# The second block's convolution placed tap by tap among the gate/up products of a two-block transformer kernel

## The chip, the cores and the metric

The kernel runs on one core of a Trainium2 chip. The metric is the device time of one execution in microseconds. The core's engines work from queues of their own, each in order: TensorE (PE, matmuls; PEld its weight loads), VectorE (DVE), ScalarE (ACT), GpSimd (POOL), and SyncE (SP), which issues the DMAs here.

## The reference

Two transformer blocks of depth 1 over 1024 tokens of width 1024, in float32. Both end in a gated feed-forward layer with D_FF = 2816 = 22 x 128:

```python
# first block
h2 = modulate(rms_norm(x, g_pre_ffn), shift_f, scale_f)
ff = (silu(h2 @ w_ffn_gate) * (h2 @ w_ffn_up)) @ w_ffn_down
# second block: a causal depthwise convolution of width 3 over the tokens between up and gate
hn = rms_norm_2(h, ffn_norm_pre)
up = causal_dwconv(hn @ w_up, conv_w, conv_b)      # y[t] = b + h[t-2]*w[0] + h[t-1]*w[1] + h[t]*w[2]
g, u = split(up, 2)
ffn = (silu(g) * u) @ w_down
```

Ahead of it stand the mixers (attention and an mLSTM in the first block, retention and sparse attention in the second), which the change does not touch.

## The kernel before

`dense` (L164) is the output projection and the feed-forward layer; it is called twice, with `conv=False` for the first block ("of1") and `conv=True` for the second ("of2"). float32 products are made from rounded parts: every operand is split into a high part (`whi`, a rounded copy made by ScalarE, L357) and a remainder (`wlo`, the difference, L358, made by the engine that the call names), and three matmuls give one product.

Gate and up are computed together, one tile f of 128 gate and 128 up columns at a time, f = 0 to 21. A tile is a 2 x 2 block product by seven multiplications in place of eight (sums of weight blocks times sums of token blocks). Multiplication m takes 12 matmuls of 512 columns; the order is 1, 6, 5, 7, 2, 3, 4, and each of these is a *slot*. The weights of the seven (`prep`, L330) need four sums on VectorE (`ws`, L344). The results lie in three PSUM banks per tile: A holds products 1 and 2, B holds 6, 7 and 4, and Z holds 5 and 3. Product 3 is added into Z, and it is the product whose moving operand is the tile `xq`. Banks are read in between by `after_product` (L380): after product 6, `u2 = t1 + B`; after product 7, `w = t1 + B` and `craw1(odd) = w + Z`; after 3, `craw0(odd) = u2 + Z`; after 4, `craw1(even) = t1 + B`. All four are VectorE additions of L378. `craw0` is the gate half before the convolution and `craw1` the up half; each is one buffer, with 512 of its elements from even and 512 from odd blocks of 128 tokens.

For the second block the convolution of tile g = f - 1 runs beside the products of tile f. `conv_start` (L437) is ScalarE's part: the newest tap with the bias, into `cv`. `conv_taps` (L443) adds the other two taps on VectorE (L448) and, for the gate half, calls SiLU on ScalarE (L450). `conv_end` (L452) multiplies the halves on VectorE (L454) and sends the result to memory (`h_d`) by SyncE. `cv0` and `cv1` have one buffer each.

The order of the work on TensorE, VectorE, ScalarE and GpSimd is the order in which the code issues it. A slot's body first issues `after_product` of the slot before, then a list of further work (`pre[i]` of slot i), then its own matmuls. In `pre`, `q(f, m, engine)` is `prep` with the engine of the remainder. With the convolution, the remainders of product 3 of this tile and of products 5 and 2 of the next are on VectorE, and the other four on GpSimd.

```python
            for fn in post:
                fn()
            post.clear()
            for fn in pre:
                fn()
            multiply(f, m, c, special)
            post.append(lambda: after_product(f, m, special, c))
```

After tile 21 follows the down projection, `down`, over groups of two tiles, a step per block of 128 tokens; its first steps issue the rest of tile 21's convolution through `tail` (L582). In the last tile's lists stand pieces of the down weights (L913) and of the first hidden tiles (L518) in place of the next tile's weights.

Of the kernel before, what the change touches and what calls it, by code (L numbers as in the profile page):

```python
# [23 lines left out]
ALU = mybir.AluOpType  # L24
# [3 lines left out]
S = 1024  # L28
D = 1024
NT = S // P  # L30
KT = D // P
NF = 22
# [8 lines left out]
C_CONV2W, C_CONV2B = 0, 3 * 2 * NF  # L41
# [45 lines left out]
class Builder:  # L87
# [76 lines left out]
    def dense(self, name, bigs, held, w0, names, x_src, x_mid, x_dst, rows, rows2, conv, ahead=None):  # L164
# [10 lines left out]
        nc = self.nc  # L175
# [8 lines left out]
        raws = []  # L184
# [3 lines left out]
        def fetch(kind, i, lags, **kw):  # L188
            W[kind, i] = self.weights_later(steps, src(kind, i), lags, **kw)
# [5 lines left out]
        def run(slots):  # L195
            for slot in slots:
                steps.run(early=True)
                slot()
                steps.run()
                steps.now += 1  # L200
# [124 lines left out]
        def raw_load(f):  # L325
            pl, tag = (px, "wx") if f % 2 else (self.wp, "raw")
            raw[f] = pl.tile([P, 2048], F32, tag=tag, bufs=1, name=tag)
            nc.sync.dma_start(raw[f], src("gu", f))
# [108 lines left out]
        def conv_start(f, j):  # L437
            col = j * NF + f
            cv = tt[f]["cv", j] = pools["v"].tile([P, S], F32, tag=f"cv{j}", bufs=1, name="cv")
            nc.scalar.activation(cv, raws[j][:, 2:], AF.Identity, scale=self.cols[:, C_CONV2W + 4 * NF + col : C_CONV2W + 4 * NF + col + 1],  # L440
                                 bias=self.cols[:, C_CONV2B + col : C_CONV2B + col + 1])

        def conv_taps(f, j):  # L443
            col = j * NF + f
            cv = tt[f]["cv", j]
            for i in (1, 0):
                wc = self.cols[:, C_CONV2W + i * 2 * NF + col : C_CONV2W + i * 2 * NF + col + 1]
                nc.vector.scalar_tensor_tensor(cv, raws[j][:, i : i + S], wc, cv, op0=ALU.mult, op1=ALU.add)  # L448
            if j == 0:
                nc.scalar.activation(cv, cv, AF.Silu)  # L450

        def conv_end(f):  # L452
            g, u = tt[f]["cv", 0], tt[f]["cv", 1]
            nc.vector.tensor_tensor(out=g, in0=g, in1=u, op=ALU.mult)  # L454
            nc.sync.dma_start(h_d[f], g)

        for tb, ps in held.items():
# [8 lines left out]
        q = lambda f, m, eng=nc.gpsimd: lambda: prep(f, m, eng)  # L466
        v = nc.vector
# [14 lines left out]
        def slot(f, m, pre=(), c=slice(0, HALF), special=False):  # L482
            def body():
# [8 lines that stand above are left out]
            return body  # L492
# [18 lines left out]
        order = (1, 6, 5, 7, 2, 3, 4)  # L511
        groups, hidden = {}, {}

        def hid_piece(f, c, hraw, eng):
            hi, lo = (hidden[f][:, i, c * HALF : (c + 1) * HALF] for i in range(2))
            s = hraw[:, c * HALF : (c + 1) * HALF]
            nc.scalar.activation(hi, s, AF.Copy)
            eng.tensor_tensor(out=lo, in0=s, in1=hi.bitcast(F32), op=ALU.subtract)  # L518
# [6 lines left out]
        def early_hid(f):  # L525
            hr = self.rows.tile([P, S], F32, tag="row", name="hraw")
            nc.sync.dma_start(hr, h_d[f])
            groups[f] = hr

        for f in range(1, NF):  # L530
            pre = [[] for _ in range(7)]
            if conv:
                g = f - 1
                pre[0] += [lambda g=g: conv_start(g, 0)]
                pre[1] += [lambda g=g: conv_taps(g, 0), lambda g=g: conv_start(g, 1)]
                pre[2] += [lambda g=g: conv_taps(g, 1)]
                pre[3] += [lambda g=g: conv_end(g)]
            if f == 1:
                pre[0] += [q(1, 2), q(1, 3), q(1, 4)]
            else:  # L540
                pre[0] += [q(f, 3, v if conv else nc.gpsimd), q(f, 4)]
            if f + 2 < NF:
                pre[1] += [lambda f=f: raw_load(f + 2)]
            if f + 1 < NF:
                for i in range(5):
                    pre[2 + i] += [q(f + 1, order[i], v if conv and i in (2, 4) else nc.gpsimd)]
            else:
                pre[1] += [lambda: [early_hid(i) for i in range(3)]]
                pre[2] += [lambda: fetch("dn", 0, (1, 2, 3, 4), lo_engine=lambda i: v if i % 2 else nc.gpsimd)]
                pre[3] += [first_hidden, lambda: hid_piece(0, 0, groups[0], v)]  # L550
                pre[4] += [lambda: hid_piece(0, 1, groups[0], nc.gpsimd), lambda: hid_piece(1, 0, groups[1], v)]
                pre[5] += [lambda: hid_piece(1, 1, groups[1], nc.gpsimd)]
                pre[6] += [lambda: early_hid(3)]
            run([slot(f, m, pre[i]) for i, m in enumerate(order)])


        f = NF - 1
# [20 lines left out]
        def both(gs, tb):  # L578
            for c in range(2):
                down(gs, tb, c)  # L580

        def tail(i):  # L582

            for fn in post:
                fn()
            post.clear()
            if conv:
                if i == 0:
                    conv_start(f, 0)
                    conv_taps(f, 0)  # L590
                    conv_start(f, 1)
                elif i == 1:
                    conv_taps(f, 1)
                    conv_end(f)
                    eso.close()
            if i == 1:
                esx.close()
                self.end_pool = pools["c"] = pools["o"] = self.pool(eso, name + "d")

# [15 lines left out]
        g = (G - 2, G - 1)  # L615
        rows2v = []
        for n in range(G - 2):
            fetch("dn", n + 1, range(4, 8))
            if n == 0:
                for i in range(4):  # L620
                    steps.at(1 + i, lambda i=i: hid_piece(2 + i // 2, i % 2, groups[2 + i // 2], v if i % 2 else nc.gpsimd), early=True)
                steps.at(7, lambda: rows2v.extend(rows2()), early=True)
            else:
                hid_later(n + 1, (0, 1, 2, 2, 4, 5))
            run([(lambda n=n, tb=tb: (tail(tb) if n == 0 and tb < 2 else None, both((n,), tb))) for tb in range(NT)])
        hid_later(g[1], (0, 1, 1, 1, 2, 3))

        def finish(tb, xin, row):
# [66 lines left out]
        n = 4  # L695
# [1503 lines left out]
```

## Time and profile before

| | us |
|---|---|
| median of 3 runs | 2982.58 (2982.33 to 2983.03) |
| the profiled execution | 2978.47 |
| its span, first to last instruction | 2976.7 |
| TensorE busy, share of the span | 2773.2, 93% |
| VectorE busy | 1733.9, 58% |
| ScalarE busy | 1148.1, 39% |
| GpSimd busy | 1228.4, 41% |
| mean granted TensorE clock | 0.968 of full speed |

The gate/up stage of the first block lies at about 880 to 1270 us of the span, that of the second at 2232 to 2720. Busy times of TensorE are modelled, since matmuls overlap; the spacing of starts is the better measure. The granted clock is given as a share of full speed (1.00 is 2.4 GHz, half of it 1.2 GHz).

### The profile page before, as it was taken

What the parts mean: (1) busy time and instruction counts of PE and PEld (TensorE: products, weight loads), DVE (VectorE), ACT (ScalarE), POOL (GpSimd) and SP (SyncE); (2) the same over time, 40 slices, a digit from 0 to 9 for tenths busy, and PEclk for the clock granted to TensorE, in tenths of its full rate; (3) what the DMA queues carried; (4) which work ended last, traced back from release to release, by engine and by line L of the source; (5) the groups of instructions that cost most, each with busy time, mean ns of one, the idle gap of its engine ahead of it and who ended that gap; (6) DMA issues with size and microseconds to landing.
All of it is one profiled execution on the core that took longest, in us unless ns stands there. A gap on an engine that the chain in (4) does not pass through costs nothing.

```text
span 2976.7 us, 41535 instructions
## 1 busy us (share of the span) xinstructions
PE 2773.2 (93%) x15792; PEld 2391.2 (80%) x15792; DVE 1733.9 (58%) x3054; ACT 1148.1 (39%) x2364; POOL 1228.4 (41%) x1127
## 2 busy tenths in 40 slices
PE   5899999999879999999989999889979988998998
PEld 5898888889768888888879999878967767776887
DVE  8635524442563344365564977865377777777556
ACT  5653223222242222321245586567343333333112
POOL 5752222244335555533364436486223222224334
PEclk7999999999989999999999999999989999999999
DMA  5112343363222222142231111121232211123322
GB/s 203 40 42 100 113 149 107 112 196 110 107 106 94 84 85 85 71 149 86 92 133 48 44 44 45 40 65 62 78 114 85 78 71 64 64 77 135 106 92 85
DMA packets 86252, 272.60 MB, mean 92 GB/s; under 512 B 9207, under 2 KB 28663, under 8 KB 71974
## 3 DMA queue, kind: packets, MB, share of 16 engines
q1 hardware_dynamic: 86054, 269.97, 25.9%
q8 instruction: 124, 2.03, 0.3%
q14 instruction: 74, 0.61, 0.1%
HBM read 210.15 MB, written 59.79 MB: 91 GB/s over the span
## 4 chain that ended last, share of the span: by engine, by line
PE 65%; DVE 19%; ACT 7%; issue 4%; POOL 4%; DMA 0%; SPq 0%; DVEq 0%; ACTq 0%; POOLq 0%
PE pd L131 12%; PE pd L132 12%; PE pd L133 12%; PE pd L375 11%; PE pa L375 8%; DVE cv L448 5%; ACT tk_junka L1651 2%; DVE ws L344 2%; DVE craw L378 1%; DVE ada_acc L826 1%; DVE xin L228 1%; PE pa L1904 1%; POOL wlo L913 1%; ACT cv L440 1%; PE pd L1877 1%
## 5 line engine op out<-in xcount | busy, mean ns | idle before, releaser
L131 PE MATMUL pd<-whi,big 128*128 128x256 f32 (+2 forms) x1856 | 554.9, 299 | 11.8 <-DVE big L574 3.8
L132 PE MATMUL pd<-wlo,big 128*128 128x256 f32 (+2 forms) x1856 | 543.9, 293 | 8.2 <-POOL wlo L913 8.2
L133 PE MATMUL pd<-whi,big 128*128 128x256 f32 (+2 forms) x1856 | 542.9, 292 | 0.9 <-POOL big L850 0.6
L913 POOL TENSOR_TENSOR wlo<-raw,whi 128x512 fp32r<-128x512 f32 (+1 forms) x254 | 351.6, 1395 | 399.1 <-ACT whi L911 381.4
L131 PEld LDWEIGHTS pd<-whi,big 128*128 128x128 f32 x1856 | 359.6, 194 | 20.8 <-ACT whi L911 4.6
L132 PEld LDWEIGHTS pd<-wlo,big 128*128 128x128 f32 x1856 | 359.9, 194 | 15.8 <-POOL wlo L913 9.9
L133 PEld LDWEIGHTS pd<-whi,big 128*128 128x128 f32 x1856 | 359.2, 194 | 6.4 <-POOL big L850 0.9
L576 DVE TENSOR_TENSOR big<-big,pd 128x512 f32<-128x512 f32 x304 | 207.4, 685 | 174.2 <-PE pd L133 172.2
L131 PE MATMUL pd<-whi,hid 128*128 128x512 f32 x576 | 228.9, 397 | 0.0
L132 PE MATMUL pd<-wlo,hid 128*128 128x512 f32 x576 | 228.3, 396 | 0.0
L133 PE MATMUL pd<-whi,hid 128*128 128x512 f32 x576 | 228.3, 396 | 0.0
L375 PE MATMUL pd<-big,whi 128*128 128x512 f32 (+1 forms) x840 | 200.6, 389 | 0.0
L375 PE MATMUL pa<-big,wlo 128*128 128x512 f32 x816 | 197.0, 390 | 1.7 <-DVE wt L378 1.7
L375 PE MATMUL pa<-big,whi 128*128 128x512 f32 x768 | 186.1, 391 | 1.7 <-ACT wlo L357 0.9
L375 PEld LDWEIGHTS pd<-big,whi 128*128 128x128 f32 x840 | 157.9, 194 | 30.8
L375 PEld LDWEIGHTS pa<-big,wlo 128*128 128x128 f32 x816 | 152.8, 188 | 35.5 <-issue 2.5
L131 PE MATMUL pd<-big,whi 128*128 128x512 f32 x448 | 180.3, 402 | 0.0
L375 PE MATMUL pd<-big,wlo 128*128 128x512 f32 x744 | 178.7, 389 | 0.0
L448 DVE SCALAR_TENSOR_TENSOR cv<-craw,cols,cv 128x1024 f32<-128x1024 f32 x88 | 156.1, 1773 | 37.6 <-ACT cv L440 36.1
L133 PE MATMUL pd<-big,wlo 128*128 128x512 f32 x448 | 175.0, 391 | 0.3 <-POOL wlo L913 0.3
L132 PE MATMUL pd<-big,whi 128*128 128x512 f32 x448 | 174.6, 390 | 0.0
L375 PEld LDWEIGHTS pa<-big,whi 128*128 128x128 f32 x768 | 145.4, 190 | 33.9 <-ACT wlo L357 2.5
(435 smaller groups left out, 5654.7 us busy)
## 6 DMA issues: line engine op xcount, KB each, us to landing
raw<-in_wu SPq DMA_DIRECT2D x87, 1024.0 KB, 4.9
wx<-in_wu SPq DMA_DIRECT2D x22, 1024.0 KB, 4.8
hraw<-of_h SPq DMA_DIRECT2D x44, 512.0 KB, 5.6
row<-in_w_ada SPq DMA_DIRECT2D x32, 512.0 KB, 3.9
x_d<-xin SPq DMA_DIRECT2D x24, 512.0 KB, 2.6
of_h<-wt SPq DMA_DIRECT2D x44, 256.0 KB, 2.0
of_h<-cv SPq DMA_DIRECT2D x22, 512.0 KB, 2.6
ada<-in_w_ada SPq DMA_DIRECT2D x16, 512.0 KB, 8.0
```

Source lines behind the costliest of these rows:

```text
L131: mm(ps, lh, rh, start=start, stop=False)
L132: mm(ps, lh, rl, start=False, stop=False)
L133: mm(ps, ll, rh, start=False, stop=stop)
L228: nc.vector.scalar_tensor_tensor(x, y, r, x, op0=ALU.mult, op1=ALU.add)
L344: nc.vector.tensor_tensor(out=t, in0=a, in1=b, op=op)
L375: nc.tensor.matmul(ps[:, c], l, r, start=first and k == 0 and i == 0, stop=k == 3 and i == 2, skip_group_check=True)
L378: nc.vector.tensor_tensor(out=out, in0=a, in1=b, op=ALU.add)
L440: nc.scalar.activation(cv, raws[j][:, 2:], AF.Identity, scale=self.cols[:, C_CONV2W + 4 * NF + col : C_CONV2W + 4 * NF + col + 1], bias=se ...
L448: nc.vector.scalar_tensor_tensor(cv, raws[j][:, i : i + S], wc, cv, op0=ALU.mult, op1=ALU.add)
L576: nc.vector.tensor_add(a, a, ps)
L913: eng.tensor_tensor(out=w[1][:, c], in0=raw[:, c], in1=w[0][:, c].bitcast(F32), op=ALU.subtract)
L1651: nc.scalar.activation(junk[:, :w], isc[tbs[i]], AF.Sign, scale=-1.0, bias=f[:, i : i + 1], accum_out=cnt[:, i : i + 1])
```

## The change

Only `dense` changes. The convolution's taps are issued one at a time (`conv_tap(f, j, i)`; j is the half, 0 gate and 1 up, i the tap), each in a slot of its own. The first half's start and first tap of tile f are issued in the last slot of the same tile, behind the addition that completes `craw0`; the start of the second half comes ahead of the first half's second tap and SiLU; the product of the halves comes one slot later, behind the addition into `craw1`, and for tile 21 on GpSimd. All remainders of gate/up weights go to GpSimd. The weights of product 3 are issued in slot 1 instead of slot 0 (in both blocks). In the last tile a piece of a hidden tile moves one slot on, and the tail spreads the rest of the convolution over four steps instead of two and closes two pools in the fourth.

```diff
-        def conv_taps(f, j):
+        def conv_tap(f, j, i):
             col = j * NF + f
             cv = tt[f]["cv", j]
-            for i in (1, 0):
-                wc = self.cols[:, ...]
-                nc.vector.scalar_tensor_tensor(cv, raws[j][:, i : i + S], wc, cv, op0=ALU.mult, op1=ALU.add)
-            if j == 0:
+            wc = self.cols[:, ...]
+            nc.vector.scalar_tensor_tensor(cv, raws[j][:, i : i + S], wc, cv, op0=ALU.mult, op1=ALU.add)
+            if (j, i) == (0, 0):
                 nc.scalar.activation(cv, cv, AF.Silu)
...
-            nc.vector.tensor_tensor(out=g, in0=g, in1=u, op=ALU.mult)
+            (nc.gpsimd if f == NF - 1 else nc.vector).tensor_tensor(out=g, in0=g, in1=u, op=ALU.mult)
...
             if conv:
                 g = f - 1
-                pre[0] += [lambda g=g: conv_start(g, 0)]
-                pre[1] += [lambda g=g: conv_taps(g, 0), lambda g=g: conv_start(g, 1)]
-                pre[2] += [lambda g=g: conv_taps(g, 1)]
-                pre[3] += [lambda g=g: conv_end(g)]
+                if g == 0:
+                    pre[0] += [lambda: conv_start(0, 0), lambda: conv_tap(0, 0, 1)]
+                pre[0] += [lambda g=g: conv_start(g, 1), lambda g=g: conv_tap(g, 0, 0)]
+                pre[1] += [lambda g=g: conv_tap(g, 1, 1)]
+                pre[2] += [lambda g=g: conv_tap(g, 1, 0)]
+                pre[4] += [lambda g=g: conv_end(g)]
+                pre[6] += [lambda f=f: conv_start(f, 0), lambda f=f: conv_tap(f, 0, 1)]
...
-                pre[0] += [q(f, 3, v if conv else nc.gpsimd), q(f, 4)]
+                pre[0] += [q(f, 4)]
+                pre[1] += [q(f, 3)]
...
-                    pre[2 + i] += [q(f + 1, order[i], v if conv and i in (2, 4) else nc.gpsimd)]
+                    pre[2 + i] += [q(f + 1, order[i])]
...
-                pre[4] += [lambda: hid_piece(0, 1, groups[0], nc.gpsimd), lambda: hid_piece(1, 0, groups[1], v)]
-                pre[5] += [lambda: hid_piece(1, 1, groups[1], nc.gpsimd)]
+                pre[4] += [lambda: hid_piece(0, 1, groups[0], nc.gpsimd)]
+                pre[5] += [lambda: hid_piece(1, 0, groups[1], v), lambda: hid_piece(1, 1, groups[1], nc.gpsimd)]
...
-            if conv:
-                if i == 0:
-                    conv_start(f, 0)
-                    conv_taps(f, 0)
-                    conv_start(f, 1)
-                elif i == 1:
-                    conv_taps(f, 1)
+            if conv and i == 0:
+                conv_start(f, 1)
+                conv_tap(f, 0, 0)
+            elif conv and i < 3:
+                conv_tap(f, 1, 2 - i)
+            elif i == 3:
+                if conv:
                     conv_end(f)
                     eso.close()
-            if i == 1:
                 esx.close()
...
-            run([(... tail(tb) if n == 0 and tb < 2 else None ...)])
+            run([(... tail(tb) if n == 0 and tb < 4 else None ...)])
```

On VectorE, in the middle of the second block's gate/up stage, these rows lead up to the addition into `craw1` that product 3 waits for (the last row). `cv` with `craw0` or `craw1` is a tap, `ws` a weight sum, `whi` or `wlo` a remainder, `wt` with `pa` one of the additions `u2` and `w`. Before, from the gate half's taps on:

```order
L358 TENSOR_TENSOR whi_22387<-ws_22388,whi_22387 128x512
L448 SCALAR_TENSOR_TENSOR cv_22385<-craw0_20973,cols_74,cv_22385 128x1024 x2
L378 TENSOR_TENSOR wt_22429<-wt_22407,pa_22416 128x512
L448 SCALAR_TENSOR_TENSOR cv_22412<-craw1_20974,cols_74,cv_22412 128x1024 x2
L454 TENSOR_TENSOR cv_22385<-cv_22385,cv_22412 128x1024
L344 TENSOR_TENSOR ws_22451<-raw_22279 128x512
L344 TENSOR_TENSOR ws_22453<-ws_22451,raw_22279 128x512
L378 TENSOR_TENSOR wt_22469<-wt_22407,pa_22416 128x512
L378 TENSOR_TENSOR craw1_20974<-wt_22469,pd_22436 128x4x128
```

The same stretch now, from the addition that completes `craw0` on:

```order
L378 TENSOR_TENSOR craw0_20973<-wt_22295,pd_22300 128x4x128
L447 SCALAR_TENSOR_TENSOR cv_22370<-craw0_20973,cols_74,cv_22370 128x1024
L378 TENSOR_TENSOR craw1_20974<-wt_22272,pa_22282 128x4x128
L447 SCALAR_TENSOR_TENSOR cv_22370<-craw0_20973,cols_74,cv_22370 128x1024
L447 SCALAR_TENSOR_TENSOR cv_22388<-craw1_20974,cols_74,cv_22388 128x1024
L344 TENSOR_TENSOR ws_22411<-wx_22144,ws_22316 128x512
L378 TENSOR_TENSOR wt_22430<-wt_22408,pa_22417 128x512
L447 SCALAR_TENSOR_TENSOR cv_22388<-craw1_20974,cols_74,cv_22388 128x1024
L344 TENSOR_TENSOR ws_22449<-raw_22280 128x512
L344 TENSOR_TENSOR ws_22451<-ws_22449,raw_22280 128x512
L378 TENSOR_TENSOR wt_22467<-wt_22408,pa_22417 128x512
L378 TENSOR_TENSOR craw1_20974<-wt_22467,pd_22436 128x4x128
```

The remainders are gone from VectorE, the gate half's first tap stands directly behind the addition into `craw0`, and the product of the halves (L454, now L453) no longer stands ahead of the last row.

On ScalarE, the same tile from the copy of bank A into `craw0` (L408) to the up half's bias part. `cv` with `craw0` or `craw1` is a bias part, `cv<-cv` the SiLU, `whi` or `wlo` the rounded copy of a weight, `wt` the copy of product 1. Before:

```order
L408 ACTIVATE craw0_20973<-pd_22394 128x4x128
L357 ACTIVATE whi_22472<-ws_22488 128x512
L357 ACTIVATE wlo_22505<-raw_22279 128x512
L440 ACTIVATE cv_22521<-craw0_20973,cols_74 128x1024
L357 ACTIVATE wlo_22505<-ws_22523 128x512
L357 ACTIVATE whi_22527<-raw_22279 128x512
L386 ACTIVATE wt_22543<-pd_22530 128x512
L450 ACTIVATE cv_22521<-cv_22521 128x1024
L440 ACTIVATE cv_22548<-craw1_20974,cols_74 128x1024
```

Now:

```order
L408 ACTIVATE craw0_20973<-pd_22395 128x4x128
L357 ACTIVATE whi_22472<-ws_22488 128x512
L440 ACTIVATE cv_22505<-craw0_20973,cols_74 128x1024
L357 ACTIVATE wlo_22508<-raw_22280 128x512
L440 ACTIVATE cv_22524<-craw1_20974,cols_74 128x1024
L449 ACTIVATE cv_22505<-cv_22505 128x1024
L357 ACTIVATE wlo_22508<-raw_22280 128x512
L386 ACTIVATE wt_22543<-pd_22530 128x512
```

Both bias parts now stand ahead of the SiLU, and the SiLU ahead of the copy of product 1.

## Rows read from the trace of the kernel before

**Rows 1.** Waits of TensorE, 2210 to 2720: us in total, times, longest.

```profile
PE pd L375 <- DVE craw L378: 54.4, 21, 5.5
```

**Rows 2.** Timeline of TensorE, second block: start, us, line, tiles, count, [idle before].

```profile
2240.65 2.88 PE L375 MATMUL pa<-big,whi 128*128 128x512 f32 x12
2243.37 2.88 PE L375 MATMUL pd<-big,whi 128*128 128x512 f32 x12
2248.27 4.61 PE L375 MATMUL pd<-xq,wlo 128*128 128x512 f32 x12 [2.02 <-DVE craw L378]
2252.72 2.92 PE L375 MATMUL pa<-big,wlo 128*128 128x512 f32 x12
...
2271.69 4.61 PE L375 MATMUL pd<-xq,whi 128*128 128x512 f32 x12 [2.45 <-DVE craw L378]
```

**Rows 3.** Timeline of TensorE, first block, one tile.

```profile
903.10 2.96 PE L375 MATMUL pd<-xq,whi 128*128 128x512 f32 x12
905.90 2.90 PE L375 MATMUL pa<-big,wlo 128*128 128x512 f32 x12
...
922.24 2.03 PE L375 MATMUL pd<-xq,whi 128*128 128x512 f32 x8
```

**Rows 4.** Windows: length, busy of PE, PEld, DVE, ACT, POOL, granted clock, DMA, GB/s.

```profile
2268.00:2278.00 10.00, 7.55 (x27) 5.74 (x26) 6.78 (x9) 3.66 (x6) 2.56 (x2) 0.83 0.31 107
2315.00:2325.00 10.00, 7.56 (x33) 5.89 (x32) 7.31 (x11) 4.03 (x6) 2.57 (x2) 1.00 0.13 53
```

**Rows 5.** Timeline around one wait, VectorE and TensorE, second block.

```profile
2403.17 3.52 DVE L448 SCALAR_TENSOR_TENSOR cv<-craw,cols,cv 128x1024 f32<-128x1024 f32 x2 [1.67 <-ACT cv L440]
...
2406.72 1.22 DVE L454 TENSOR_TENSOR cv<-cv 128x1024 f32<-128x1024 f32 x1
...
2409.91 0.69 DVE L378 TENSOR_TENSOR craw<-wt,pd 128x512 f32<-128x512 f32 x1
...
2410.65 3.06 PE L375 MATMUL pd<-xq,wlo 128*128 128x512 f32 x12 [2.44 <-DVE craw L378]
```

**Rows 6.** Timeline of TensorE, the last tile and the tail.

```profile
2712.04 4.92 PE L375 MATMUL pd<-xq,wlo 128*128 128x512 f32 x12 [5.51 <-DVE craw L378]
2716.80 2.93 PE L375 MATMUL pa<-big,wlo 128*128 128x512 f32 x12
...
2731.64 0.50 PE L131 MATMUL pd<-whi,big 128*128 128x512 f32 x1 [3.76 <-DVE big L574]
```

**Rows 7.** Groups by line, 2240 to 2700: count, busy us, mean ns, idle before.

```profile
L440 ACT ACTIVATE cv<-craw,cols 128x1024 f32<-128x1024 f32 x40 | 49.5, 1238 | 39.5 <-DVE craw L378 39.5
L378 DVE TENSOR_TENSOR craw<-wt,pd 128x512 f32<-128x512 f32 x40 | 27.5, 689 | 50.0 <-PE pd L375 42.8 <-ACT whi L357 6.5
L358 POOL TENSOR_TENSOR whi<-ws,whi 128x512 fp32r<-128x512 f32 x20 | 25.7, 1284 | 64.0 <-ACT whi L357 54.3 <-issue 9.7
L454 DVE TENSOR_TENSOR cv<-cv 128x1024 f32<-128x1024 f32 x20 | 24.5, 1225 | 0.7
L358 DVE TENSOR_TENSOR whi<-ws,whi 128x512 fp32r<-128x512 f32 x20 | 20.3, 1016 | 7.3 <-ACT whi L357 7.3
L344 DVE TENSOR_TENSOR ws<-wx 128x512 f32<-128x512 f32 x20 | 13.6, 682 | 0.0
```

**Rows 8.** Timeline, taps of one tile: beside a remainder on GpSimd, and alone.

```profile
2397.21 1.29 POOL L358 TENSOR_TENSOR whi<-raw,whi 128x512 fp32r<-128x512 f32 x1 [6.07 <-ACT whi L357]
2397.25 2.33 DVE L448 SCALAR_TENSOR_TENSOR cv<-craw,cols,cv 128x1024 f32<-128x1024 f32 x1
...
2399.62 1.28 DVE L448 SCALAR_TENSOR_TENSOR cv<-craw,cols,cv 128x1024 f32<-128x1024 f32 x1
```

**Rows 9.** DMA issues, 2240 to 2700: queue, count, KB each, us to landing.

```profile
wx<-in_wu SPq DMA_DIRECT2D x10, 1024.0 KB, 4.9
of_h<-cv SPq DMA_DIRECT2D x20, 512.0 KB, 2.6
```

More of the change, by code (lines that the diff above doesn't have):

```diff
@@ L441, in conv_start @@
                                  bias=self.cols[:, C_CONV2B + col : C_CONV2B + col + 1])
-        def conv_taps(f, j):
+        def conv_tap(f, j, i):
             col = j * NF + f
             cv = tt[f]["cv", j]
-            for i in (1, 0):
-                wc = self.cols[:, C_CONV2W + i * 2 * NF + col : C_CONV2W + i * 2 * NF + col + 1]
-                nc.vector.scalar_tensor_tensor(cv, raws[j][:, i : i + S], wc, cv, op0=ALU.mult, op1=ALU.add)
-            if j == 0:
+            wc = self.cols[:, C_CONV2W + i * 2 * NF + col : C_CONV2W + i * 2 * NF + col + 1]
+            nc.vector.scalar_tensor_tensor(cv, raws[j][:, i : i + S], wc, cv, op0=ALU.mult, op1=ALU.add)
+            if (j, i) == (0, 0):
                 nc.scalar.activation(cv, cv, AF.Silu)
@@ L624, in dense @@
                 hid_later(n + 1, (0, 1, 2, 2, 4, 5))
-            run([(lambda n=n, tb=tb: (tail(tb) if n == 0 and tb < 2 else None, both((n,), tb))) for tb in range(NT)])
+            run([(lambda n=n, tb=tb: (tail(tb) if n == 0 and tb < 4 else None, both((n,), tb))) for tb in range(NT)])
         hid_later(g[1], (0, 1, 1, 1, 2, 3))
```

## The prediction

> **What bounds the kernel now.** I read the page first (TensorE is busy for nearly the whole span, so the question is where it stands still), then the list of who waited for whom in the second block's gate/up stage, then TensorE's timeline of that stage beside the same stage of the first block, and last VectorE's rows around one wait.
>
> In the second block's stage TensorE waits 21 times for one and the same writer, VectorE's addition into `craw` [rows 1]: once for each of the tiles f = 1 to 21, always at the matmuls that read `xq`, which is product 3. Product 3 accumulates into bank Z, and the addition that reads Z for output quadrant 21 (`plus(odd(raws[1]), ...)`, after product 7) must have read it first. The reader is to see two things in the timeline [rows 2]: most products follow each other at 2.72 us, but product 3 begins about 2.45 us late in every tile, and it then often lasts 4.45 us. The first block runs the same seven products without a convolution, and there a tile takes 922.24 - 903.10 = 19.14 us, its product 3 taking 2.80 [rows 3]. So the long product 3 is a second cost of the wait: in a window that holds it the granted clock is 0.83 of full speed, one part of it at 1.2 instead of 2.4 GHz, while TensorE had just stood still; a window with another such wait shows 1.00 [rows 4]. The length of a tile shows that some waits cost the clock and some do not.
>
> Why the addition is late is seen on VectorE [rows 5]: it comes last in a queue of two pairs of taps, the product of the halves and two weight sums, with no pause ahead of it. VectorE is the bound of this stage, and through a chain: the taps wait for ScalarE's bias part, and the next bias part for the taps.
>
> **The change part by part.**
>
> *The loop.* From product 3 of f = 1 at 2248.27 to that of f = 21 at 2712.04 are 20 tiles in 463.77 us [rows 2, 6], 23.19 each. If TensorE never waits, they take 20 x 19.14 = 382.8. That is 80.97 to gain, and whether it comes is a question of one addition: when is `craw1` written? I lay out VectorE's new order with the durations of [rows 7], zero being the end of product 3. Product 4 then ends at 2.72, 1 at 5.44, 6 at 8.16, 5 at 10.88, 7 at 13.60, and product 2 at 16.32, where product 3 wants its bank.
>
> Addition into `craw0` 0.69; ScalarE's bias part 1.24, to 1.93; first tap 1.28, to 3.21; addition into `craw1` 0.69, to 3.90; second tap to 5.18; first tap of the other half to 6.46 (its bias part ran on ScalarE beside the second tap); a weight sum 0.68, to 7.14; then the addition that needs product 6, from 8.16 to 8.84; last tap to 10.12; two weight sums to 11.48; the addition that needs product 7, from 13.60 to 14.28; the addition into `craw1` to 14.97. It is wanted at 16.32. So VectorE is 1.35 us early, and it stands idle twice on the way (1.02 before product 6, 2.12 before product 7). The product of the halves, which stood ahead of this addition, now stands behind it and ends at 16.2; the sum for product 7 follows, to 16.9, and 19.12 starts the next round. Three remainders (1.02 us on average for those cut from a sum) have left VectorE.
>
> *The price of those three on GpSimd.* GpSimd takes 1.28 us for one [rows 7], seven in a tile are 9 of 19.1 us, so it has the time. But the two engines get in each other's way: a tap takes 1.28 us alone and 2.33 beside a remainder on GpSimd [rows 8], 1.05 more. In the stretch to 13.60 stand the remainders of 2, 4, 3 and the next 1, four of them. Without a hit the addition is 1.35 early; if all four hit a tap or a sum it is later by 4.2, less the idle time it finds on the way. Two hits before 8.16 cost 2.10 - 1.02 = 1.08, two more after it 2.10, which ends the sums at 14.66 instead of 11.48, and `craw1` at 16.03, still 0.3 early; a fifth hit, by a remainder left over from the tile before, makes it 17.1, so 0.8 late. I take zero, since five hits in five are not likely and the additions that read PSUM keep their 0.69 throughout [rows 7]; the bound is 0.8 us a tile, and with it the clock again (1.65).
> The Trainium skill (SBUF — State Buffer, "SBUF: two separate sides") speaks against the change here: VectorE and GpSimd share a pair of ports as an exclusive lock, and whoever comes second is blocked for the whole instruction. The trace agrees in kind (1.05 of a 1.29 us instruction); by the rule all seven remainders could block VectorE in turn, which is the first rival below.
>
> *First and last tile.* At f = 1, product 2 starts at 2243.37 and product 3 at 2248.27 instead of 2.72 later: 2.18 to gain [rows 2]. The new order there puts ScalarE's SiLU ahead of three copies for the weights, which can hold the copy of product 1 and with it product 7; from nothing to 1.4 us, an estimate from the taps ahead of it (two at 1.28 to 2.33); I take 0.5. At f = 21, product 3 lasts 4.76 us instead of 2.80: 1.96 to gain [rows 6]. Its wait of 5.51 is inside the 20 tiles. Two instructions on VectorE (a remainder of the down weights, one of the hidden tile) take the place of the sums, 0.68 to 1.73 us each (a sum's time, with a hit or without), which brings `craw1` to 15.0 at best and 17.1 at worst: nothing taken.
>
> *The tail.* Behind f = 21 TensorE waits 3.76 us for a copy out of PSUM that stands behind taps and the product of the halves [rows 6]. The taps are now spread over three steps of 2.72 us with two copies of about 0.69 in each, and the product is on GpSimd. Per step VectorE has 1.4 for the copies, 1.28 to 2.33 for a tap and in two steps 0.7 to 1.7 more: 2.7 to 5.4 against 2.72, with banks for some two steps of delay. The remaining wait lies between 0 and 3.8; I take 2, a gain of 1.8.
>
> *First block.* The remainder for product 3 moves one product later there too, still four products ahead of its use; TensorE has no wait in that stage [rows 3], whose rows follow each other at 2.72 to 2.80. Nothing, with a bound of 1 us either way for the order of GpSimd's work. The later closing of pools at both tails issues nothing; SyncE's queue keeps its order but for one load. Nothing.
>
> Sum: 80.97 + 2.18 - 0.5 + 1.96 + 1.8 = 86.4. The profiled execution took 2978.47, so 2892.1; the median of the runs shown lies 4.1 above it, and the forecast for a median is 2896.
>
> **The rivals.**
>
> *VectorE stays the bound, by GpSimd.* For it: the 2.33 above, three more remainders in a tile, and a VectorE that was the bound. Against it: the 3.1 us of idle time in the layout. VectorE's own work in a tile is four taps 5.12, the product 1.23, four sums 2.72 and five additions 3.45, together 12.5; with seven hits of 1.05 and 1.33 for the first bias part it is 21.2. A tile that long has a wait of 2.1, and with the clock's 1.65 takes 22.9: hardly a gain, 2896 + 20 x 3.7 = 2970. With the bound of four hits (0.8 late) it is 2896 + 16 = 2912, or 2945 where the clock falls too. By the Trainium skill's rule (the page named above), seven whole instructions of 1.29 in place of seven waits of 1.05 give a tile of 24.5, 2896 + 20 x 5.4 = 3004; since no row shows more than 1.05 and most of the trace's remainders meet nothing, that has 0.01 of this rival's chance.
>
> *The output tile's copy to memory.* `cv0` has one buffer. The new bias part of the first half is issued only two products behind the product of the halves, and has to wait until that result is in memory. The copy lands 2.6 us after its issue [rows 9]: 16.2 + 2.6 = 18.8, and the bias part wants to start at 19.12 + 0.69 = 19.8. That is 1.0 us of slack (before, it had two products more). If the weights' load of 1024 KB, 4.9 us [rows 9], ran into it, the copy would land at 23.7, or at 24.7 with a hit on the product; ScalarE would stand 3.9 to 4.9 us with VectorE's first tap behind it, and after the 1.35 of slack product 3 would wait 2.5 to 3.6 us: a tile of 23.3 to 24.4, clock included, against 23.19. The ends give back 5.4, so it is 2979 to 3001, slower from a wait of 2.7 us in every tile; I price it at 3.35, 2996. Against it: by the layout GpSimd has the remainders of 4 and 3 at about 10, when SyncE issues the load, which has landed at 15.
>
> *Little changes.* The wait is only traded for another of the same length (a bank, a weight): 2975 to 2988. The even waits of [rows 1], one writer alone, speak against it.
>
> **How the numbers follow.** The forecast 0.75 (2888 to 2906 by itself: the tail and the first tile between their bounds), VectorE by GpSimd 0.17, the copy 0.03, little changes 0.03, and 0.02 for more than I count. The range, 2889 to 2930, takes in the forecast and the milder half of the first rival. A difference of 0.2% (6 us) is what a measurement here can tell from none: faster 0.95, the same 0.02, slower 0.03.
>
> **What would show it.** Right: in the second block's stage a tile takes 19.1 us, TensorE's list of waits there has no addition into `craw` any more, the granted clock is 1.00, and the addition into `craw1` ends a little over 1 us before product 3. The gaps at 2248 and 2712 are gone; that behind f = 21 is under 3.8. Wrong: `xq` rows that still start late; then taps of 2.3 us standing beside most remainders are the first rival, and a bias part on ScalarE that waits for a copy is the second.

## The result, and the profile after

The changed kernel takes 2893.56 us (median of four runs, 2891.78 to 2897.18) against 2982.57, a ratio of 0.9703 (95% interval 0.9686 to 0.9720). The forecast was 2896. The profiled execution took 2897.18 us, its span is 2895.4.

TensorE's list of waits in the second block's gate/up stage and the stage ahead of it (line waited for: us in total, times, longest) no longer has the 21 waits of [rows 1]:

```profile
PE pd L375 <- ACT wx L357: 5.6, 1, 5.6
PE pa L300 <- DVE big L304: 5.2, 3, 2.5
...
PE pa L375 <- DVE wt L378: 1.7, 2, 0.9
PE pd L375 <- ACT big L303: 1.1, 1, 1.1
PE pd L375 <- DVE big L304: 0.3, 1, 0.3
```

What is left stands in tile 0 and in the turning of the inputs ahead of it. TensorE's timeline (start, us, line, operation, count), at tile 1, at one tile in the middle and at tile 21, answers to [rows 2] and [rows 6]:

```profile
2251.40 2.88 PE L375 MATMUL pd<-big,whi 128*128 128x512 f32 x12
2254.12 3.01 PE L375 MATMUL pd<-xq,wlo 128*128 128x512 f32 x12
2256.97 2.92 PE L375 MATMUL pa<-big,wlo 128*128 128x512 f32 x12
...
2464.74 2.96 PE L375 MATMUL pd<-xq,whi 128*128 128x512 f32 x12
...
2483.88 2.49 PE L375 MATMUL pd<-xq,wlo 128*128 128x512 f32 x10
...
2636.99 3.03 PE L375 MATMUL pd<-xq,wlo 128*128 128x512 f32 x12
2639.86 2.92 PE L375 MATMUL pa<-big,wlo 128*128 128x512 f32 x12
2642.62 0.39 PE L131 MATMUL pd<-whi,big 128*128 128x512 f32 x1
```

Product 3 follows product 2 after 2.72 us everywhere, and the tile in the middle takes 2483.88 - 2464.74 = 19.14 us, as in the first block [rows 3]. From tile 1 to tile 21 it is 2636.99 - 2254.12 = 382.87, where it was 463.77. In the tail TensorE has no wait at all; the list for that stretch is empty, and from product 4 of tile 21 to the end it is 255.5 us against 259.9. Two windows of the stage (columns as in [rows 4]) show TensorE without a pause at the full clock, while VectorE works 122 of 150 us:

```profile
2350.00:2500.00 150.00, 150.00 (x660) 123.51 (x659) 122.12 (x110) 66.89 (x94) 89.72 (x55) 1.00 0.23 85
2500.00:2650.00 150.00, 150.00 (x660) 123.36 (x659) 122.67 (x115) 70.40 (x102) 86.33 (x54) 1.00 0.26 95
```

VectorE's timeline of the tile whose product 3 ends at 2467.70 (2464.74 + 2.96) can be laid beside the order worked out in the prediction:

```profile
2467.80 0.69 DVE L378 TENSOR_TENSOR craw<-wt,pd 128x512 f32<-128x512 f32 x1 [0.97 <-PE pd L375]
2469.81 1.28 DVE L447 SCALAR_TENSOR_TENSOR cv<-craw,cols,cv 128x1024 f32<-128x1024 f32 x1 [1.31 <-ACT cv L440]
2471.01 0.68 DVE L378 TENSOR_TENSOR craw<-wt,pa 128x512 f32<-128x512 f32 x1
2471.61 2.91 DVE L447 SCALAR_TENSOR_TENSOR cv<-craw,cols,cv 128x1024 f32<-128x1024 f32 x2
2474.44 0.68 DVE L344 TENSOR_TENSOR ws<-wx,ws 128x512 f32<-128x512 f32 x1
2475.99 0.69 DVE L378 TENSOR_TENSOR wt<-wt,pa 128x512 f32<-128x512 f32 x1 [0.86 <-ACT wlo L357]
2476.59 2.06 DVE L447 SCALAR_TENSOR_TENSOR cv<-craw,cols,cv 128x1024 f32<-128x1024 f32 x1
2478.58 1.77 DVE L344 TENSOR_TENSOR ws<-raw 128x512 f32<-128x512 f32 x1
2480.39 0.69 DVE L344 TENSOR_TENSOR ws<-ws,raw 128x512 f32<-128x512 f32 x1
2481.36 0.69 DVE L378 TENSOR_TENSOR wt<-wt,pa 128x512 f32<-128x512 f32 x1 [0.28 <-PE pa L375]
2482.08 0.69 DVE L378 TENSOR_TENSOR craw<-wt,pd 128x512 f32<-128x512 f32 x1
2482.68 1.52 DVE L453 TENSOR_TENSOR cv<-cv 128x1024 f32<-128x1024 f32 x1
```

The addition into `craw1` (2482.08) ends at 2482.77, 15.07 us after the zero; the layout said 14.97. Product 3 reads its bank at 2483.88, so 1.11 us are left, where 1.35 were foreseen. The pauses have shrunk from 1.02 and 2.12 to 0.86 and 0.28, since a tap (0.44 in the pair, 0.78 alone) and a sum (1.08) were held up by GpSimd: 2.3 us ahead of the addition, and the pauses took up 2.0 of them. (Behind the addition the product and the next sum lose another 1.4.) How they are held up is seen beside GpSimd's rows of the same stretch:

```profile
2476.28 1.30 POOL L358 TENSOR_TENSOR wlo<-ws,wlo 128x512 fp32r<-128x512 f32 x1
2477.53 2.27 POOL L358 TENSOR_TENSOR whi<-raw,whi 128x512 fp32r<-128x512 f32 x1
```

The last tap (2476.59) starts beside the first of these remainders and ends at 2478.65, 1.07 us behind it. The second remainder starts beside the tap and ends at 2479.80, 1.15 us behind it; the sum (2478.58) ends at 2480.35, 0.55 us behind that. So each takes about its own time (1.28, 1.28, 0.69) from where the other is through.

From tile 2 to tile 20 the addition ends 1.10 to 1.11 us ahead of product 3. At the two ends it is much closer: 0.10 us ahead at tile 1, and 0.15 at tile 21, where it ends 16.03 us after the zero (rows of the two additions, to be held against product 3 at 2254.12 and 2636.99):

```profile
2253.33 0.69 DVE L378 TENSOR_TENSOR craw<-wt,pd 128x512 f32<-128x512 f32 x1
2636.16 0.69 DVE L378 TENSOR_TENSOR craw<-wt,pd 128x512 f32<-128x512 f32 x1
```

The taps' mean in the stage fell, from 1775 to 1578 ns, though more remainders run on GpSimd, and the copy to memory lands as before [rows 9] (line groups, the first of before and the others of after, then DMA issues of after):

```profile
L448 DVE SCALAR_TENSOR_TENSOR cv<-craw,cols,cv 128x1024 f32<-128x1024 f32 x80 | 142.0, 1775 | 34.8 <-ACT cv L440 33.3
L447 DVE SCALAR_TENSOR_TENSOR cv<-craw,cols,cv 128x1024 f32<-128x1024 f32 x80 | 124.7, 1578 | 26.7 <-ACT cv L440 26.7
L358 POOL TENSOR_TENSOR whi<-ws,whi 128x512 fp32r<-128x512 f32 x39 | 60.1, 1546 | 30.8 <-ACT whi L357 30.8
```

```profile
of_h<-cv SPq DMA_DIRECT2D x19, 512.0 KB, 2.6
```

A remainder on GpSimd now takes 1.55 us or more on average, 1.28 before [rows 7]: the two engines hold each other up, in both directions.

### The profile page after: what moved, and what is told of

Same layout as the page of the kernel before. It is cut to its first block, busy times and chain, and to the rows that moved or that the text cites. A ratio compares the mean times of both kernels' runs of the same rounds, so it can differ in the third digit from the quotient of the medians.

```text
span 2895.4 us, 41559 instructions
## 1 busy us (share of the span) xinstructions
PE 2745.5 (95%) x15792; PEld 2377.1 (82%) x15792; DVE 1731.3 (60%) x2993; ACT 1152.3 (40%) x2364; POOL 1349.5 (47%) x1188
## 4 chain that ended last, share of the span: by engine, by line
PE 76%; DVE 11%; ACT 5%; POOL 4%; issue 3%; DMA 0%; SPq 0%; DVEq 0%; ACTq 0%; POOLq 0%
PE pd L375 16%; PE pd L131 13%; PE pd L132 13%; PE pd L133 13%; PE pa L375 12%; ACT tk_junka L1653 2%; DVE ada_acc L828 1%; PE pa L1906 1%; POOL wlo L915 1%; DVE xin L228 1%; PE pd L1879 1%; PE pd L1603 1%; POOL rs_r L148 1%; DVE cv L1229 1%; POOL sws L1090 1%
## 5 line engine op out<-in xcount | busy, mean ns | idle before, releaser
L358 POOL TENSOR_TENSOR wlo<-ws,wlo 128x512 fp32r<-128x512 f32 x90 | 127.7, 1424 | 116.7 <-ACT wlo L357 116.6
L131 PE MATMUL pd<-big,whi 128*128 128x512 f32 x448 | 180.3, 402 | 0.0
L378 DVE TENSOR_TENSOR wt<-wt,pa 128x512 f32<-128x512 f32 x110 | 75.6, 688 | 169.6 <-PE pa L375 111.3
L358 POOL TENSOR_TENSOR whi<-ws,whi 128x512 fp32r<-128x512 f32 x84 | 118.6, 1417 | 123.0 <-ACT whi L357 123.0
```

What stands on the lines that cost most here:

```text
L131: mm(ps, lh, rh, start=start, stop=False)
L358: eng.tensor_tensor(out=w[:, 1], in0=s, in1=w[:, 0].bitcast(F32), op=ALU.subtract)
L378: nc.vector.tensor_tensor(out=out, in0=a, in1=b, op=ALU.add)
```

## The experiments

The theory: one thing ends the waits, an addition into `craw1` that comes in time. The parts that could bring it are the product of the halves, moved behind the addition; the taps and bias parts, taken apart and moved ahead; and the three remainders, taken off VectorE. The rival was that one of these alone does it, or that one of them costs.

**Remainders alone.** Before, and:

```diff
-                pre[0] += [q(f, 3, v if conv else nc.gpsimd), q(f, 4)]
+                pre[0] += [q(f, 3), q(f, 4)]
-                    pre[2 + i] += [q(f + 1, order[i], v if conv and i in (2, 4) else nc.gpsimd)]
+                    pre[2 + i] += [q(f + 1, order[i])]
```

> The kernel before with one edit: all remainders of gate/up weights on GpSimd. Theory (the wait is the end of VectorE's chain from the addition into craw0 to the one into craw1): of the three remainders only the one for product 3 stands inside that chain, 0.69 us and some 0.76 of waiting for ScalarE; 2.6 - 1.45 leaves a wait of about 1.2 us, a tile of 20.3, or 22.0 where the clock falls too, and 2982.6 - 20 x (23.19 - 20.3 or 22.0) = 2925 to 2959. Rival A (VectorE was simply overloaded, and three remainders fewer are the gain): a tile of 19.1 and about 2900. Rival B (GpSimd's hits eat it): no faster than before.

2924.38 us, ratio 0.9814 (0.9798 to 0.9830). TensorE's waits in 200 us:

```profile
PE pd L375 <- DVE craw L378: 9.0, 10, 0.9
```

Each of ten tiles still waits 0.9 us, and takes 20.31 to 20.33; the product after the wait follows at 2.9 us, so the clock stays. This is 57 us (2981.20, the kernel before on the same chip, less 2924.38), nearly two thirds of the gain of 89, from a part that, as the next run shows, the changed kernel can do without.

**The order alone.** The changed kernel with the remainders of products 3, 5 and 2 back on VectorE:

```diff
-                pre[1] += [q(f, 3)]
+                pre[1] += [q(f, 3, v if conv else nc.gpsimd)]
-                    pre[2 + i] += [q(f + 1, order[i])]
+                    pre[2 + i] += [q(f + 1, order[i], v if conv and i in (2, 4) else nc.gpsimd)]
```

> The changed kernel with the remainders of products 3, 5 and 2 of the second block back on VectorE. Theory: the new order alone is enough; VectorE had 1.1 us to spare ahead of product 3 and 0.9 and 0.3 of idle time before it, against one remainder of 0.7 plus a wait for ScalarE inside the chain, and GpSimd's hits are fewer: tiles of 19.14, time within 4 us of the changed kernel, 2890 to 2898. Rival A (relief of VectorE is what counts): tiles above 20, over 2915.

2891.94 us, ratio 0.9703 (0.9689 to 0.9717): no different from the whole change. The window shows why (columns as above): TensorE is never idle, and VectorE with its three remainders works 153 of 200 us. The addition into `craw1` ends 15.07 us after the zero here too.

```profile
2300.00:2500.00 200.00, 200.00 (x880) 164.69 (x879) 152.63 (x180) 87.31 (x124) 58.51 (x43) 1.00 0.23 85
```

**The product alone.** Before, with the product of the halves one slot later:

```diff
-                pre[3] += [lambda g=g: conv_end(g)]
+                pre[4] += [lambda g=g: conv_end(g)]
```

> The kernel before with one edit: the product of the halves is issued one slot later, behind the addition into craw1. Theory: the chain loses the product's 1.22 us, the wait falls from 2.6 to about 1.4, a tile is 20.5, or 22.2 where the clock falls: 2929 to 2963. Rival (the product was hidden behind something else): no change, 2978 to 2983.

2928.74 us, ratio 0.9826 (0.9812 to 0.9841); the wait is 1.2 us in each tile of 20.6:

```profile
PE pd L375 <- DVE craw L378: 12.1, 10, 1.2
```

So taking 1.22 us [rows 5] from ahead of the addition shortens the wait by about as much (2.44 to 1.2) and gives 52 us in all (2981.20 less 2928.74), since the clock no longer falls either.

**Product and remainders together**, both edits on before.

> The kernel before with two edits: the product one slot later and all remainders on GpSimd; the taps stay in pairs and the bias parts where they were. Theory: 2.6 - 1.22 - 1.45 is below zero, so the wait is gone without the taps being spread: tiles of 19.14 with under half a us to spare, and only the first tile and the tail stay as before: 2897 to 2905. Rival (the single taps and the bias parts ahead are what does it): a wait of a us or more, tiles of 20 to 22, over 2915.

2902.11 us, ratio 0.9737 (0.9723 to 0.9752). TensorE's list of waits has none from tile 2 to tile 20, and these tiles take 19.22 to 19.26 us. The rest of the gain, some 10 us (2902.11 less 2891.94 of the order alone), lies mostly at the ends: a wait of 0.80 at tile 1, of 1.99 at tile 21, with a slow product of 4.60 us behind it, and of 3.75 in the tail; tiles longer by 0.1 us are some 2 us of it. Spreading the taps is thus not needed for the loop; the ends are mended by the rest of the new order, of which only the tail's steps were run apart. What the spread taps give with the product left in its old place, no run shows.

**The changed kernel again**, on one chip with the kernels of the last slot, the tail and the first block.

> The changed kernel once more, unedited, beside the next ones: a measure of how far two profiles of it differ. Both theories: 2891 to 2897, tiles of 19.14. Ahead of the second block's gate/up stage its first profile ran 5.2 us later than the kernel before, which no term of the prediction covers; if that was scatter, this profile is off by another amount, and if it belongs to the change, by about the same.

2892.18 us (2890.18 to 2896.08), ratio 0.9706 (0.9692 to 0.9719). The first matmuls on `xq` in the stage start at 2213.44 us of its span, in the first profile at 2214.46, before at 2209.28: 4.2 us later than before, where the first profile was 5.2 later, so most of it comes with the change.

**The product in the last slot.** The changed kernel with one edit:

```diff
-                pre[4] += [lambda g=g: conv_end(g)]
-                pre[6] += [lambda f=f: conv_start(f, 0), lambda f=f: conv_tap(f, 0, 1)]
+                pre[6] += [lambda g=g: conv_end(g), lambda f=f: conv_start(f, 0), lambda f=f: conv_tap(f, 0, 1)]
```

> The changed kernel with the product of the halves issued in the last slot, right ahead of the next tile's bias part, so that the copy of cv0 to memory stands in front of that bias part. Theory (the copy rival, which needed about 1 us more than there was): the product ends 2.0 to 3.1 us after product 3, its copy lands 2.6 later, the bias part starts at 4.6 to 5.7 in place of 0.8; of the 3.8 to 4.9 us the chain finds 0.9 + 0.3 idle and 1.1 spare, so product 3 waits 1.5 to 2.6 us: tiles of 20.7 to 21.8, up to 23.4 with the clock; 2924 to 2980. Rival (only the product's 1.22 us joins the chain, the copy costs nothing): tiles of 19.14 and no wait.

2945.01 us (one run); a tile takes 21.41 to 21.47. In 200 us ScalarE and TensorE wait:

```profile
ACT cv L440 <- DMA of_h<-cv: 58.9, 10, 5.9
```

```profile
PE pa L375 <- DVE wt L378: 14.4, 10, 1.5
PE pd L375 <- DVE craw L378: 2.6, 9, 0.3
```

The prediction's second rival, made to happen: the bias part waits 5.9 us for `cv0` to be in memory, VectorE's first tap behind it comes late, and TensorE waits 1.44 us at product 7 and 0.28 at product 3 (the wait was foreseen at product 3 alone). The mechanism is real; in the changed kernel it doesn't occur, where ScalarE's list of waits in the same stretch has no DMA in it.

**Three more sums.** The changed kernel with three repeated weight sums (0.69 us each) a tile on VectorE, ahead of the addition into `craw1`:

```diff
                 sums[f, 6] = sub(sums[f, 5], a11)
+                if conv and f > 1:
+                    for _ in range(3):
+                        nc.vector.tensor_tensor(out=sums[f, 6], in0=sums[f, 5], in1=a11, op=ALU.subtract)
```

> The changed kernel with three more weight sums (repeats, 0.68 us each) on VectorE in every tile of the second block's gate/up stage, ahead of the addition into craw1. Measures the slack: 2.04 us more, of which the idle time before the addition takes 0.28 and the slack at product 3 1.11, so a wait of about 0.7 us, a tile of 19.8 to 20.4, and 2905 to 2920 in all. Rival, the slack is an accident of one tile and VectorE is at its bound: each sum costs its whole 0.68, a tile over 21, above 2930.

2935.57 us (one run). The tiles are not alike: 20.2 to 22.6 us. Most have the wait foreseen, 0.34 to 0.99; seven of 21 have 1.97 to 2.50. Two of the former and one of the latter on TensorE, and the instruction on ScalarE that explains it:

```profile
2444.16 3.04 PE L378 MATMUL pd<-xq,wlo 128*128 128x512 f32 x12 [0.67 <-DVE craw L381]
2464.55 3.04 PE L378 MATMUL pd<-xq,whi 128*128 128x512 f32 x12 [0.99 <-DVE craw L381]
2486.90 4.39 PE L378 MATMUL pd<-xq,whi 128*128 128x512 f32 x12 [2.50 <-DVE craw L381]
```

```profile
2470.98 1.25 ACT L443 ACTIVATE cv<-craw,cols 128x1024 f32<-128x1024 f32 x1 [2.42 <-DMA of_h<-cv]
```

The slack of 1.1 us was right, but it is not the only one. The sums push the product of the halves back too; it ends at 2466.19 there, and its copy to memory releases the bias part at 2470.98, 4.8 us later where 2.6 is usual. So a second limit lies about as near as the first, the copy's, and six of the seven long waits come through it: in the tile ahead of each the bias part waits 1.6 to 2.6 us for the copy. The seventh is at tile 1, where the changed kernel has only 0.10 us to spare. Why the copy lands late in those tiles stays open; a load beside it, as the second rival had it, is not the cause in the tile shown, where the queues moved 0.54 MB from 2462 to 2472, little more than the copy itself. Five of those seven bring the slow product as well (4.39 to 4.62 us). The total lies where the rival put it, but not for its reason: the tiles without a late copy wait as the theory had it.

**Remainders doubled.** The changed kernel with the remainders of products 1 to 4 computed twice on GpSimd in the second block's stage:

```diff
-            eng.tensor_tensor(out=w[:, 1], in0=s, in1=w[:, 0].bitcast(F32), op=ALU.subtract)
+            for _ in range(2 if conv and f > 1 and m in (1, 2, 3, 4) else 1):
+                eng.tensor_tensor(out=w[:, 1], in0=s, in1=w[:, 0].bitcast(F32), op=ALU.subtract)
```

> The changed kernel with the remainders of products 1, 2, 3 and 4 computed twice on GpSimd in the second block's stage: 11 of them a tile, 14 us of GpSimd's 19.1. Theory (a hit costs VectorE up to 1.05 us, and the idle time and the slack take 2.25): with four more hits 4.2 - 2.25, a tile of up to 21.1, most likely 20.4. Rival, hits are rare and short in the mean: no wait, 19.14 a tile, 2892.

2925.46 us (one run); 17 of 20 tiles take 20.6 to 20.7. GpSimd is busy 189 of 200 us, VectorE 182:

```profile
PE pd L376 <- DVE craw L379: 6.8, 10, 0.7
PE pa L376 <- DVE wt L379: 4.1, 10, 1.4
...
2300.00:2500.00 200.00, 189.02 (x807) 149.53 (x806) 181.78 (x136) 80.33 (x116) 188.83 (x106) 1.00 0.22 79
```

VectorE has the same work in a tile, and its tiles are longer, yet it is busy for 182 us of 200, where the changed kernel has 122 of 150, or 163 of 200: the difference is time in which GpSimd held it up. TensorE waits for VectorE's additions alone, for no remainder. This is the prediction's first rival, made to happen by four more remainders: with 11 in a tile VectorE is the bound, with seven it is not.

**The tail as before.** The changed kernel with the tail in two steps, the last product of the halves on VectorE, and the pools of both blocks closed in the second step:

```diff
-            (nc.gpsimd if f == NF - 1 else nc.vector).tensor_tensor(out=g, in0=g, in1=u, op=ALU.mult)
+            nc.vector.tensor_tensor(out=g, in0=g, in1=u, op=ALU.mult)
...
-            elif conv and i < 3:
-                conv_tap(f, 1, 2 - i)
-            elif i == 3:
+            elif i == 1:
                 if conv:
+                    conv_tap(f, 1, 1)
+                    conv_tap(f, 1, 0)
                     conv_end(f)
```

> The changed kernel with the tail in two steps again: both taps of the up half and the product of the halves, on VectorE, in the second step. Theory: the wait for a copy out of PSUM behind tile 21 comes back, 3 to 4 us, and nothing else: 2896 to 2899. Rival (the wait went because VectorE comes to the tail earlier, not because of the steps): under 1 us, as the changed kernel.

2895.70 us, ratio 0.9717 (0.9704 to 0.9730), 3.5 us above the changed kernel beside it (2892.18). The tail's wait is back, at 2.45 us, a little less than the 3 to 4 expected:

```profile
PE pd L131 <- DVE big L577: 2.5, 1, 2.5
```

In the profile the tail costs 3.0 us more than in the changed kernel. The profiled execution is shorter all the same (2895.22 to 2896.08), because this kernel's second mixer was 3.2 us shorter, which the next runs look into. The run packs the steps and moves the product back to VectorE at once, so it doesn't tell these two apart.

**The first block as before.** The changed kernel, but with the order of the weights, of the hidden piece and of the tail's steps in the first block as before.

> The changed kernel with the first block as it was before (weights of product 3 in slot 0 ahead of those of 4, the hidden piece in slot 4, the pools closed in the tail's second step). Theory (the first block's part is worth nothing, and the 3 us that the changed kernel and the run with placement alone lose in the second block's mixer at about 1820 to 1900 are scatter): within 2 us of the changed kernel run beside it. Rival (closing the pools later moves the next mixer's tiles and costs 3 us there): 3 us faster than the changed kernel, and its profile starts the second gate/up stage where the kernel before does.

2888.14 us (2887.11 to 2890.50), ratio 0.9691 (0.9678 to 0.9704), on the chip on which the changed kernel took 2892.18: 4.0 us less, which is the rival's side.

**Only the pools closed early**, in the first block's tail:

```diff
-            elif i == 3:
+            elif i == (3 if conv else 1):
...
-            run([(... tail(tb) if n == 0 and tb < 4 else None ...)])
+            run([(... tail(tb) if n == 0 and tb < (4 if conv else 2) else None ...)])
```

> The changed kernel with one difference: in the first block's tail the pools are closed at the second step (i == 1) as before, not at the fourth. Theory of the pools: the 3.2 us that the changed kernel loses in the second block's mixer go with the closing, so 2889 (2892.2 less 3.2). Rival, the order of the remainder and the hidden piece in the first block does it: no difference, 2892. In the trace the theory expects no wait of 2 us of TensorE at the row that reads `ro` near 1817 and no interval of half clock near 1874.

2892.85 us (2888.03 to 2897.14), ratio 0.9705 (0.9691 to 0.9718). In the trace the 3.2 us are gone, in the median they are not. The windows of the two places in the second block's mixer, first of the changed kernel's second profile, then of this one:

```profile
1810.00:1825.00 15.00, 12.97 (x109) 12.63 (x109) 8.47 (x33) 5.71 (x12) 9.93 (x13) 1.00 0.35 106
1870.00:1880.00 10.00, 8.31 (x55) 7.91 (x55) 7.63 (x25) 8.85 (x18) 3.96 (x5) 0.83 0.31 107
```

```profile
1810.00:1825.00 15.00, 14.23 (x118) 13.65 (x117) 9.41 (x36) 7.68 (x16) 11.49 (x16) 1.00 0.34 107
1870.00:1880.00 10.00, 9.04 (x76) 8.95 (x76) 6.68 (x23) 8.78 (x20) 2.34 (x3) 1.00 0.31 107
```

The first loss is a wait of ScalarE, for a transfer by the profile, the same instruction in the one and in the other:

```profile
1816.67 0.38 ACT L1805 ACTIVATE rsq<-pd 128x256 f32<-128x256 f32 x1 [3.46 <-DMA ret_d<-ryt]
```

```profile
1814.67 0.38 ACT L1805 ACTIVATE rsq<-pd 128x256 f32<-128x256 f32 x1 [1.67 <-DMA ret_d<-ryt]
```

The second is a stretch of lower clock near 1874, 0.83 against 1.00.

**The first block as before, again.**

> The changed kernel with the first block wholly as before, a second time. If leaving the first block alone is worth its 4 us (2888.14 against 2892.18 on one chip, while closing the pools early alone gave 2892.85), it comes to 2887 to 2890 again. Rival, executions scatter by some us whatever the kernel (before: 2978.56 to 2983.60 in nine) and the first time was a low draw: 2891 to 2894.

2890.62 us (2887.27 to 2893.70), ratio 0.9699 (0.9686 to 0.9712): between the two expectations. The ten runs of this kernel, on two chips, have a mean of 2889.5, and the eight of the changed kernel one of 2893.3. It is likely the best of all, by some 4 us, but the intervals of the ratios overlap, so that it beats the changed kernel isn't proven; that it beats the kernel before is.

## Why the prediction was right

**The loop** (80.97 us predicted) gave 463.77 - 382.87 = 80.90. The mechanism is the one foreseen, an addition that comes in time. That its end was right to 0.1 us is a weak test, though: the last two additions start when product 7 ends, at 13.60, so any order that is ready by then gives the same end, as the order alone does. What the layout had too large is the pause ahead of product 7, 2.12 us where 0.28 were left, because it took zero for GpSimd's hits. There are 2.3 us of hits ahead of the addition, and nearly all of them fall into the pauses, as the bound with four hits had it. So the loop could have lost 1.4 us more in a tile (0.28 and the 1.11 behind the addition) before a wait, not the 3.5 of the layout.

By the rule of the Trainium skill (SBUF — State Buffer, "SBUF: two separate sides"), that VectorE and GpSimd block each other for whole instructions, the prediction's estimate of a tile was 24.5 us; it is 19.14. The trace agrees with the blocking (the tap, the remainders and the sum at 2476.28 to 2480.35, each through before the other goes on), and the additions that read PSUM kept their 0.69 us. What was too high is the step from there to 24.5: not every remainder meets one of VectorE's instructions, one that does costs only what is left of it (0.44, 0.78 and 1.08 us here), and pauses take that up.

**The remainders** were given a price but no use of their own: the prediction counted their 3 us off VectorE into the layout and did not ask whether the layout stood without them. It does (the order alone: 2891.94). The loop is settled twice over: by the product and the remainders together, or by the new order (the product's new place included) without the remainders.

**Tile 1** gave the whole 2.18 (18.62 to 16.44 us from tile 0's product 4 to product 3); the 0.5 set aside for ScalarE's SiLU ahead of the copies did not occur. **Tile 21**: 1.96 predicted, 4.76 - 2.87 = 1.89 measured; the addition came at 16.03, in the middle of the 15.0 to 17.1 foreseen. Both terms came whole by a margin of 0.10 and 0.15 us, which is partly luck.

**The tail** was the term that was mis-sized: 1.8 predicted, 4.4 measured. The step that failed is the delay of 2 us left for the taps in the steps; the list of waits there is empty, so that the whole 3.76 came, with 0.6 more. With the old tail 2.45 us of the wait and 3.0 of the time come back, so that much belongs to the spread steps and the product on GpSimd, which no run tells apart; the other 1.3 of the wait went with the rest of the change.

**The pools.** That "the later closing of pools at both tails issues nothing", and so costs nothing, is what the traces contradict. All six profiles with the later closing in the first block (the changed kernel twice, the order alone, the product in the last slot, the three more sums, the doubled remainders) lose 3.0 to 3.3 us of TensorE's time between about 1804 and 1906 us against before. Of the seven that close in the second step, six (the remainders alone, product and remainders, the old tail, the first block as before twice, the pools alone) lose or gain under 0.2, and the product alone loses 1.6, nearly all of it in the stretch of lower clock (0.90 from 1870 to 1880). So the wait of some 1.7 us near 1815 goes with the later closing, while the clock's share, 1.5, also comes without it. The prediction looked for instructions and found none; that the closing moves where later tiles lie, and so what they wait for, would explain it but isn't shown. Which transfer or tile it is, the runs don't settle, and the medians of the pools-alone kernel don't show the gain. Another 2.7 us of the changed kernel's profiled execution lie near 2215, in a stretch with a granted clock of 0.81 where before had 1.00; these come and go between executions of one kernel (with the first block as before, that window has 0.89 in the one profile and 1.00 in the other).

So the profiled execution fell by 81.3 us (2978.47 to 2897.18) where 86.4 were summed up: the loop and the ends gave 89.4, the rest of the program took 8 back, 5.9 of it at the two places named. That the median still came within 2.4 us of the forecast is partly luck: the 4.1 us added for the step from a profiled execution to a median have the wrong sign for this kernel, whose profiled execution is the slowest of its four runs.

**The rivals.** Both are mechanisms of this kernel, as the doubled remainders and the product in the last slot show, and both lie near: VectorE's chain has 1.4 us to spare in the tile shown, and the copy 0.8 (issued at 2484.23, 2.6 to land, the bias part at 2487.67). Neither decides at the order chosen.

## What to carry to other kernels

Lay the busy engine's instructions of one tile out against the times at which the other engine frees and wants its banks, pauses included: here that told that the deciding addition comes in time and what the pauses could absorb. Look at the pauses left, and not only at the end: an addition that starts when a product ends comes at the same time whether 2.1 us or 0.3 are left ahead of it. Before counting two edits of a change as both needed, ask whether the layout stands with one of them; here 57 and 52 us came from either of two small edits alone, and the two together gave nearly all of the loop. And when one limit has about 1 us of slack, look at the next one: three sums of 0.69 us ran into two limits at once.

## What was not expected of the hardware

A wait of 0.9 to 1.2 us in every tile left the granted clock at 1.00 (the remainders alone and the product alone, 200 us each), and so did two waits of 1.4 and 0.3 (the product in the last slot). Waits of 2.0 to 2.5 us were followed by a slow product of 4.4 to 4.6 us in five of seven cases with the three more sums, and in 15 of the first 20 in the kernel before. So each of the small edits got back, beside its own share of the wait, what the clock had cost (1.65 us in a tile that paid it).
